# The weights of a row norm, its epsilons and the sums of its shares go from GpSimd to VectorE; GpSimd keeps the power

## The chip, the cores and the metric

The kernel runs on one core of one Trainium2 chip. The metric is the device time of one launch in microseconds (us), the median over runs; lower is better. The core has five engines that each work through a queue of their own, in the order in which it was written: TensorE (PE in the profile; PEld is its loading of weights), VectorE (DVE), ScalarE (ACT), GpSimd (POOL) and SyncE (SP), which here issues the DMAs. An engine starts its next instruction when the semaphores that this instruction waits for have been raised by others.

## The reference

A decoder trunk of two layers over 512 tokens, 1024 wide, all in float32. Each layer runs four parts in a row, and each part takes a row norm before and after:

```python
def rmsnorm(x, g):
    y = xf * lax.rsqrt(jnp.mean(xf * xf, axis=-1, keepdims=True) + RMS_EPS)
    return (y * g.astype(jnp.float32)).astype(x.dtype)

    f = swiglu(rmsnorm(h, g[0]), ...)          # gated FFN, 2816 wide
    h = h + FFN_RES_WEIGHT * rmsnorm(f, g[1])
    m_in = rmsnorm(h, g[2])                    # layer 0: retention, layer 1: stick-breaking attention
    h = h + rmsnorm(m, g[3])
    f = swiglu(rmsnorm(h, g[4]), ...)
    h = h + FFN_RES_WEIGHT * rmsnorm(f, g[5])
    gate = jax.nn.sigmoid(rmsnorm(h, g[6]) @ ple_w_gate[i])
    h = h + rmsnorm(gate * e, g[7])            # e: the layer's own input embedding, projected
```

So there are eight junctions in the program at which a part ends, is normed and added to the stream (the post norm and the residual), and the sum is normed again for the next part (the pre norm). After the last part there is no pre norm. Retention also norms each head, with an epsilon of its own.

## The kernel before

The 512 tokens are four blocks of 128 (t = 0 to 3), one token per partition. `part[t]` (in the rows below `part_92` to `part_95`, or `part`) holds a part's output of 128x1024 for block t, in two column halves a and b of 512. Matmuls run in float32r, each operand split into a high and a low piece (`wh` and `wl` for weights, `xs` for the turned input): ScalarE writes the high piece (L153), VectorE the low one (L150), and a product is three matmuls (L158 to L160, or L713 inside the FFN).

The end of a part is its *tail*. For each block the last matmuls of half a and then half b fall into PSUM (`ps`). What follows for block t, in the names used below:

- add a, add b (L552, L559 on VectorE): the half from PSUM is added into `part[t]`. In the input-embedding part, called PLE from here, a product with the sigmoid stands in their place (L1184).
- square a (L518, ScalarE): squares of half a with their row sum `ss`. Then, in `post_a`, epsilon a (L520) and weight a (L522), both on GpSimd: the epsilon is added to the sum, and half a is multiplied by the norm's weights `gbc`.
- square b (L532, ScalarE), weight b (L533, VectorE), and in `post_b` on GpSimd the sum of the two shares (L534) and the power -1/2 (L535).
- residual (L540, VectorE): `part[t]` times that power plus the old stream `rin`.
- the pre norm in `pre`: the square of the whole row (L459, ScalarE), epsilon and power in `rstd` (L450, L451, GpSimd), and the scaling into `xn` (L464, VectorE).
- turning: eight transposes of `xn` on TensorE (L471), then high and low pieces into `xs` (L153, L150).

In an FFN's tail the matmuls of a and b alternate block by block, twelve each. In retention and stick-breaking attention the four halves a are closed first, one after the other, and then half b block by block. In PLE half a comes from a product that is done before the tail, and the tail loads its weights (`blk<-raw`, home blocks) as it starts. Transposes of blocks 0 and 1 stand in TensorE's queue inside the tail, behind the matmuls of block 2 and behind the half a of block 3 (in retention and attention at the corresponding places), those of blocks 2 and 3 between matmuls of the next part on blocks 0 and 1.

The order of each queue is made when the program is built. TensorE's is the order of the code (`manual_schedule`). On the other engines a list scheduler picks by priority; everything in a tail stands in `chained` regions with high priority, and these tie the tail's instructions on VectorE, ScalarE and GpSimd to the order in which the code names them. So where the code names an instruction is where it stands in its engine's queue.

`rstd` is also called in retention for each head and block (L898 gives it a variance); there it stands between VectorE's statistics and a product on GpSimd (L902).

Of the kernel before, what the change touches and what calls it, by code (L numbers as in the profile page):

```python
# [15 lines left out]
ALU = mybir.AluOpType  # L16
# [13 lines left out]
RMS_EPS = 1e-6  # L30
# [47 lines left out]
class Trunk:  # L78
# [367 lines left out]


    def rstd(self, ss, eps):
        r = self.st()
        self.nc.gpsimd.tensor_scalar(out=r, in0=ss, scalar1=1.0, scalar2=eps, op0=ALU.mult, op1=ALU.add)  # L450
        self.power = self.nc.gpsimd.tensor_tensor(out=r, in0=r, in1=self.mhalf, op=ALU.pow)  # L451
        return r

# [58 lines left out]
    def post_a(self, t, g, half):  # L512

        nc = self.nc
        k = 1.0 / 16 if half else 1.0 / 32
        ss = self.st()
        a = self.part[t][:, :512]
        nc.scalar.activation(self.junk, a, AF.Square, scale=k, accum_out=ss)  # L518
        r = self.st()
        nc.gpsimd.tensor_scalar(out=r, in0=ss, scalar1=1.0, scalar2=(4 if half else 1) * RMS_EPS,  # L520
                                op0=ALU.mult, op1=ALU.add)
        nc.gpsimd.tensor_tensor(out=a, in0=a, in1=g[:, :512], op=ALU.mult)  # L522
        return r

    def post_b(self, t, g, half, ssa, after):


        nc = self.nc
        k = 1.0 / 16 if half else 1.0 / 32
        ss, r = self.st(), self.st()  # L530
        b = self.part[t][:, 512:]
        nc.scalar.activation(self.junk, b, AF.Square, scale=k, accum_out=ss)  # L532
        nc.vector.tensor_tensor(out=b, in0=b, in1=g[:, 512:], op=ALU.mult)  # L533
        nc.gpsimd.tensor_tensor(out=r, in0=ss, in1=ssa, op=ALU.add)  # L534
        nc.gpsimd.tensor_tensor(out=r, in0=r, in1=self.mhalf, op=ALU.pow)  # L535

        def residual():
            rin = self.rins.pop(0)
            for c in (slice(0, 512), slice(512, D)) if self.halves else (slice(0, D),):
                nc.vector.scalar_tensor_tensor(out=self.part[t][:, c], in0=self.part[t][:, c], scalar=r,  # L540
                                               in1=rin[:, c], op0=ALU.mult, op1=ALU.add)
            if t + 2 < NT:
                self.fetch_res(t + 2)
            after(t)

        self.todo_c.append(residual)
# [774 lines left out]
```

## Time and profile before

| | us |
|---|---|
| median of 3 runs | 2278.73 (2278.62 to 2280.29) |
| the profiled execution, its own time | 2279.08 |
| its span, first to last instruction | 2276.3 |
| TensorE busy | 2194.0 (96%) |
| VectorE busy | 1480.5 (65%) |
| ScalarE busy | 1004.3 (44%) |
| GpSimd busy | 236.0 (10%) |
| mean granted TensorE clock | 0.988 |

How to read the rows: a timeline row is start, duration, engine, line, operation, output and inputs, shape, count, and in brackets the idle time of the engine ahead of it with what ended it. A row of the view of groups has the count, the busy time, the mean in ns, and the idle time ahead. In the view of waits stand who waited for whom, us in total, times and the longest. A row of the view by windows has the stretch, its length, then the busy time (and number) on PE, PEld, DVE, ACT and POOL, the granted clock (1.00 is full), the share of the DMA engines and GB/s. ACTIVATION_READ_ACCUMULATOR is the end of a square: it writes the row sum.

### The profile page before, as it was taken

The numbers are of one execution on the slowest core, as the hardware profiler recorded it, in microseconds if no ns is written. First come the engines' busy times: TensorE is split into PE (matmuls) and PEld (weight loads), VectorE is DVE, ScalarE is ACT, GpSimd is POOL, SyncE is SP. The second block draws the span as 40 slices with busy tenths as digits, with TensorE's granted clock in tenths as the row PEclk, the third lists the DMA queues.
The fourth block names the chain that finished last, engine by engine and source line by source line (L and its number), as shares of the span: only waits on it lengthen the run. The fifth ranks groups of instructions, "written<-read, shape, count | busy, mean of one in ns | idle before, by whom it ended". The sixth has DMA issues, their size and how long they took to land.

```text
span 2276.3 us, 33005 instructions
## 1 busy us (share of the span) xinstructions
PE 2194.0 (96%) x13640; PEld 1974.0 (87%) x13640; DVE 1480.5 (65%) x1739; ACT 1004.3 (44%) x1468; POOL 236.0 (10%) x337
## 2 busy tenths in 40 slices
PE   7999999999999999999989999999999989999988
PEld 6999998888888899999868999998888889999976
DVE  7977666553544587766667877567554578776664
ACT  5544443332232355444454544344555445444452
POOL 0000002211111300000131000002221220000022
PEclk9999999999999999999999999999999999999999
DMA  5432335232222423323443332335212233332341
GB/s 208 130 111 94 99 125 166 79 116 75 97 75 67 159 94 121 103 93 102 148 153 126 109 113 94 102 113 170 78 58 73 84 112 111 103 102 93 126 134 56
DMA packets 69414, 248.81 MB, mean 109 GB/s; under 512 B 7952, under 2 KB 7952, under 8 KB 69264
## 3 DMA queue, kind: packets, MB, share of 16 engines
q1 hardware_dynamic: 69264, 246.72, 32.9%
q8 instruction: 106, 1.74, 0.3%
q14 instruction: 44, 0.36, 0.0%
HBM read 229.38 MB, written 17.30 MB: 108 GB/s over the span
## 4 chain that ended last, share of the span: by engine, by line
PE 85%; DVE 7%; ACT 3%; POOL 2%; issue 1%; DMA 1%; SPq 0%; DVEq 0%; POOLq 0%; ACTq 0%
PE ps L713 35%; PE ps L159 16%; PE ps L160 16%; PE ps L158 16%; PE ps L1018 1%; DVE part L540 1%; ACT xn L459 1%; POOL st L535 1%; DVE xs L150 1%; DVE wl L150 1%; DMA raw<-wts 1%; ACT wh L153 1%; ACT junk L532 1%; DVE xn L464 1%; POOL st L534 1%
## 5 line engine op out<-in xcount | busy, mean ns | idle before, releaser
L150 DVE TENSOR_TENSOR wl<-raw,wh 128x1024 fp32r<-128x1024 f32 x435 | 537.1, 1237 | 425.3 <-ACT wh L153 422.9
L153 ACT ACTIVATE wh<-raw 128x1024 fp32r<-128x1024 f32 x435 | 460.9, 1060 | 726.4 <-PE ps L160 229.3
L713 PE MATMUL ps<-xs,wh 128*128 128x256 f32 x2560 | 462.8, 282 | 0.0
L713 PEld LDWEIGHTS ps<-xs,wh 128*128 128x128 f32 x2560 | 399.1, 189 | 4.3 <-DVE y L676 0.2
L713 PE MATMUL ps<-xs,wl 128*128 128x256 f32 x1280 | 362.7, 283 | 0.0
L713 PE MATMUL ps<-xe,wh 128*128 128x256 f32 x1920 | 348.6, 283 | 0.0
L713 PEld LDWEIGHTS ps<-xe,wh 128*128 128x128 f32 x1920 | 300.3, 192 | 1.2
L158 PE MATMUL ps<-wh,blk 128*128 128x512 f32 x744 | 291.6, 392 | 1.5 <-DVE blk L904 1.5
L160 PE MATMUL ps<-wh,blk 128*128 128x512 f32 x744 | 291.1, 391 | 0.5 <-DVE blk L150 0.5
L159 PE MATMUL ps<-wl,blk 128*128 128x512 f32 x744 | 291.4, 392 | 0.0
L713 PE MATMUL ps<-xe,wl 128*128 128x256 f32 x960 | 271.6, 283 | 0.0
L713 PEld LDWEIGHTS ps<-xs,wl 128*128 128x128 f32 x1280 | 241.5, 189 | 0.0
L159 PE MATMUL ps<-xs,wh 128*128 128x256 f32 (+1 forms) x576 | 189.0, 328 | 12.4 <-DVE xs L150 12.4
L158 PE MATMUL ps<-xs,wh 128*128 128x256 f32 (+1 forms) x576 | 189.8, 329 | 4.7 <-ACT xs L153 4.7
L160 PE MATMUL ps<-xs,wl 128*128 128x256 f32 (+1 forms) x576 | 187.8, 326 | 0.0
L713 PEld LDWEIGHTS ps<-xe,wl 128*128 128x128 f32 x960 | 183.9, 192 | 0.0
L160 PEld LDWEIGHTS ps<-wh,blk 128*128 128x128 f32 x744 | 140.1, 188 | 30.6 <-DVE blk L150 0.9
L158 PEld LDWEIGHTS ps<-wh,blk 128*128 128x128 f32 x744 | 140.2, 188 | 29.1 <-DVE blk L904 1.9
L159 PEld LDWEIGHTS ps<-wl,blk 128*128 128x128 f32 x744 | 140.3, 189 | 27.1
L158 PE MATMUL ps<-wh,xs 128*128 128x512 f32 (+1 forms) x448 | 162.7, 363 | 0.1
L160 PE MATMUL ps<-wh,xs 128*128 128x512 f32 (+1 forms) x448 | 162.5, 363 | 0.0
L159 PE MATMUL ps<-wl,xs 128*128 128x512 f32 (+1 forms) x448 | 162.4, 363 | 0.0
(163 smaller groups left out, 3236.1 us busy)
## 6 DMA issues: line engine op xcount, KB each, us to landing
raw<-wts SPq DMA_DIRECT2D x382, 512.0 KB, 3.5
keep<-part SPq DMA_DIRECT2D x28, 512.0 KB, 4.4
rin<-keep SPq DMA_DIRECT2D x28, 512.0 KB, 4.1
gbc<-gains SPq DMA_DIRECT2D x16, 512.0 KB, 3.8
part<-x SPq DMA_DIRECT2D x4, 512.0 KB, 7.6
rin<-x SPq DMA_DIRECT2D x4, 512.0 KB, 5.3
out<-part SPq DMA_DIRECT2D x8, 256.0 KB, 2.1
dec<-decay SPq DMA_DIRECT2D x4, 256.0 KB, 3.9
```

Source lines behind the costliest of these rows:

```text
L150: eng.tensor_tensor(out=out, in0=x, in1=h, op=ALU.subtract)
L153: self.nc.scalar.activation(hl[0], x, AF.Copy)
L158: mm(ps, a[0], b[0], start=start, stop=False)
L159: mm(ps, a[0], b[1], start=False, stop=False)
L160: mm(ps, a[1], b[0], start=False, stop=stop)
L459: a = nc.scalar.activation(xn, self.part[t], AF.Square, scale=1.0 / 32, accum_out=ss)
L464: v = nc.vector.scalar_tensor_tensor(out=xn, in0=self.part[t], scalar=r, in1=g, op0=ALU.mult, op1=ALU.mult)
L532: nc.scalar.activation(self.junk, b, AF.Square, scale=k, accum_out=ss)
L534: nc.gpsimd.tensor_tensor(out=r, in0=ss, in1=ssa, op=ALU.add)
L535: nc.gpsimd.tensor_tensor(out=r, in0=r, in1=self.mhalf, op=ALU.pow)
L540: nc.vector.scalar_tensor_tensor(out=self.part[t][:, c], in0=self.part[t][:, c], scalar=r, in1=rin[:, c], op0=ALU.mult, op1=ALU.add)
L713: nc.tensor.matmul(o, w[a][:, g, k, :], x[b][:, k, :], start=new and g + k + n == 0, stop=k == 3 and n == 2, skip_group_check=True)
```

## The change

`post_a`'s product with the weights, every epsilon, and the sum of the two shares are issued to VectorE; the multiplication by one in front of each epsilon goes. In `post_a` the product now stands ahead of the epsilon. GpSimd keeps the power alone (and retention's own products and the masks of attention, which the change doesn't touch). `post_b` gets its sum and power through `rstd`.

```diff
     def rstd(self, ss, eps):
+
         r = self.st()
-        self.nc.gpsimd.tensor_scalar(out=r, in0=ss, scalar1=1.0, scalar2=eps, op0=ALU.mult, op1=ALU.add)
+        if isinstance(eps, float):
+            self.nc.vector.tensor_scalar(out=r, in0=ss, scalar1=eps, scalar2=None, op0=ALU.add)
+        else:
+            self.nc.vector.tensor_tensor(out=r, in0=ss, in1=eps, op=ALU.add)
         self.power = self.nc.gpsimd.tensor_tensor(out=r, in0=r, in1=self.mhalf, op=ALU.pow)
         return r
...
         nc.scalar.activation(self.junk, a, AF.Square, scale=k, accum_out=ss)
         r = self.st()
-        nc.gpsimd.tensor_scalar(out=r, in0=ss, scalar1=1.0, scalar2=(4 if half else 1) * RMS_EPS,
-                                op0=ALU.mult, op1=ALU.add)
-        nc.gpsimd.tensor_tensor(out=a, in0=a, in1=g[:, :512], op=ALU.mult)
+        nc.vector.tensor_tensor(out=a, in0=a, in1=g[:, :512], op=ALU.mult)
+        nc.vector.tensor_scalar(out=r, in0=ss, scalar1=(4 if half else 1) * RMS_EPS, scalar2=None, op0=ALU.add)
         return r
...
-        ss, r = self.st(), self.st()
+        ss = self.st()
         b = self.part[t][:, 512:]
         nc.scalar.activation(self.junk, b, AF.Square, scale=k, accum_out=ss)
         nc.vector.tensor_tensor(out=b, in0=b, in1=g[:, 512:], op=ALU.mult)
-        nc.gpsimd.tensor_tensor(out=r, in0=ss, in1=ssa, op=ALU.add)
-        nc.gpsimd.tensor_tensor(out=r, in0=r, in1=self.mhalf, op=ALU.pow)
+        r = self.rstd(ss, ssa)
```

The order on TensorE and SyncE stays as it was, row by row. On VectorE it changes in every tail. This is VectorE's queue in the tail of layer 0's second FFN, from block 0's half b to block 1's residual; first before, with the engine that each row waits for (Activation is ScalarE):

```order
L559 TENSOR_TENSOR part_92<-part_92,ps 128x512 [waits PE_49]
L533 TENSOR_TENSOR part_92<-part_92,gbc 128x512 [waits Activation_49]
L540 SCALAR_TENSOR_TENSOR part_92<-part_92,st,rin 128x1024 [waits DVE_49,Pool_49]
L552 TENSOR_TENSOR part_93<-part_93,ps 128x512 [waits PE_49]
L559 TENSOR_TENSOR part_93<-part_93,ps 128x512 [waits PE_49]
L533 TENSOR_TENSOR part_93<-part_93,gbc 128x512 [waits Activation_49]
L464 SCALAR_TENSOR_TENSOR xn<-part_92,st,gbc 128x1024 [waits Pool_49]
L540 SCALAR_TENSOR_TENSOR part_93<-part_93,st,rin 128x1024 [waits DVE_49,Pool_49]
```

and the same stretch in the changed program, whose line numbers are two to four higher:

```order
L561 TENSOR_TENSOR part_92<-part_92,ps 128x512 [waits PE_49]
L536 TENSOR_TENSOR part_92<-part_92,gbc 128x512 [waits Activation_49]
L454 TENSOR_TENSOR st<-st 128x1
L542 SCALAR_TENSOR_TENSOR part_92<-part_92,st,rin 128x1024 [waits Pool_49]
L452 TENSOR_SCALAR st<-st 128x1 [waits Activation_49]
L554 TENSOR_TENSOR part_93<-part_93,ps 128x512 [waits PE_49]
L524 TENSOR_TENSOR part_93<-part_93,gbc 128x512 [waits Activation_49]
L525 TENSOR_SCALAR st<-st 128x1
L561 TENSOR_TENSOR part_93<-part_93,ps 128x512 [waits PE_49]
L536 TENSOR_TENSOR part_93<-part_93,gbc 128x512 [waits Activation_49]
L454 TENSOR_TENSOR st<-st 128x1
L468 SCALAR_TENSOR_TENSOR xn<-part_92,st,gbc 128x1024 [waits Pool_49]
```

Between block 0's residual (L542) and block 1's add a (L554) there now stands the pre norm's epsilon (L452), which waits for ScalarE; and between add a and add b stand weight a and epsilon a, which wait for ScalarE too.

The second place is the start of layer 0's PLE tail, where four products with the sigmoid (`part<-blk`) are followed by the low pieces of the tail's weights (`blk<-raw,blk`, eight halves). Before:

```order
L1184 TENSOR_TENSOR part_94<-blk 128x512 [waits Activation_49]
L1184 TENSOR_TENSOR part_95<-blk 128x512 [waits DMAHW7_49,Activation_49]
L150 TENSOR_TENSOR blk<-raw,blk 128x512 [waits Activation_49] x4
L150 TENSOR_TENSOR blk<-raw,blk 128x512 [waits DMAHW5_49,Activation_49]
L150 TENSOR_TENSOR blk<-raw,blk 128x512 [waits Activation_49]
```

and now:

```order
L1186 TENSOR_TENSOR part_94<-blk 128x512 [waits Activation_49]
L524 TENSOR_TENSOR part_92<-part_92,gbc 128x512 [waits DMAHW6_49,Activation_49]
L525 TENSOR_SCALAR st<-st 128x1
L1186 TENSOR_TENSOR part_95<-blk 128x512 [waits DMAHW7_49,Activation_49]
L150 TENSOR_TENSOR blk<-raw,blk 128x512 [waits Activation_49]
L524 TENSOR_TENSOR part_93<-part_93,gbc 128x512 [waits Activation_49]
L525 TENSOR_SCALAR st<-st 128x1
L150 TENSOR_TENSOR blk<-raw,blk 128x512 [waits Activation_49]
```

The four weights a and epsilons a, which GpSimd worked through beside these rows, now stand among them. Outside the tails the scheduler moved a few rows past their neighbours at the start of three FFNs and once inside attention.

## The prediction

> **What bounds the kernel now.** First the page's shares and its chain of waits:
>
> ```profile
> PE 2194.0 (96%) x13640; PEld 1974.0 (87%) x13640; DVE 1480.5 (65%) x1739; ACT 1004.3 (44%) x1468; POOL 236.0 (10%) x337
> PE 85%; DVE 7%; ACT 3%; POOL 2%; issue 1%; DMA 1%; SPq 0%; DVEq 0%; POOLq 0%; ACTq 0%
> ```
>
> TensorE bounds it, and its work isn't changed. So the edit counts only where TensorE stands and waits for the norms. The view of waits names those places:
>
> ```profile
> PE ps L471 <- DVE xn L464: 27.2, 12, 8.1
> PE ps L159 <- DVE xs L150: 12.4, 8, 3.0
> ```
>
> The first row is the transposes that wait for the scaled row. The timelines of four FFN tails and of attention's tail show where it arises:
>
> ```profile
> 373.56 1.09 PE L471 MATMUL ps<-ident,xn 128*128 128x128 f32 x8 [2.08 <-DVE xn L464]
> 1144.20 1.09 PE L471 MATMUL ps<-ident,xn 128*128 128x128 f32 x8 [2.06 <-DVE xn L464]
> 1574.04 1.09 PE L471 MATMUL ps<-ident,xn 128*128 128x128 f32 x8 [2.08 <-DVE xn L464]
> 2198.23 1.09 PE L471 MATMUL ps<-ident,xn 128*128 128x128 f32 x8 [2.03 <-DVE xn L464]
> 1833.39 1.94 PE L471 MATMUL ps<-ident,xn 128*128 128x128 f32 x8 [3.50 <-DVE xn L464]
> ```
>
> In every FFN tail TensorE stands 2.0 to 2.1 us ahead of block 1's transposes: there the norm chain, not TensorE, sets the pace, and each us added to that chain is a us of the run.
>
> **The FFN tail.** The chain from block 0's residual to block 1's scaling, in the tail at 1130 us:
>
> ```profile
> 1130.61 1.28 DVE L540 SCALAR_TENSOR_TENSOR part<-part,st,rin 128x1024 f32<-128x1024 f32 x1 [0.71 <-POOL st L535]
> 1131.81 0.68 DVE L552 TENSOR_TENSOR part<-part,ps 128x512 f32<-128x512 f32 x1
> 1131.93 1.06 ACT L459 ACTIVATE xn<-part 128x1024 f32<-128x1024 f32 x1 [2.75 <-DVE part L540]
> 1132.90 0.18 ACT L459 ACTIVATION_READ_ACCUMULATOR xn<-part 128x1 f32 x1
> 1132.99 0.62 ACT L518 ACTIVATE junk<-part 128x512 bf16<-128x512 f32 x1
> 1133.51 0.19 ACT L518 ACTIVATION_READ_ACCUMULATOR junk<-part 128x1 f32 x1
> 1134.65 1.31 DVE L533 TENSOR_TENSOR part<-part,gbc 128x512 f32<-128x512 f32 x1 [0.85 <-ACT junk L532]
> 1135.88 1.27 DVE L464 SCALAR_TENSOR_TENSOR xn<-part,st,gbc 128x1024 f32<-128x1024 f32 x1
> 1136.08 1.48 POOL L535 TENSOR_TENSOR st<-st,mhalf 128x1 f32<-128x1 f32 x1
> 1137.60 1.29 DVE L540 SCALAR_TENSOR_TENSOR part<-part,st,rin 128x1024 f32<-128x1024 f32 x1 [0.44 <-POOL st L535]
> 1142.87 1.27 DVE L464 SCALAR_TENSOR_TENSOR xn<-part,st,gbc 128x1024 f32<-128x1024 f32 x1
> ```
>
> Before, VectorE runs add a (1131.81) while ScalarE squares the row, and epsilon a and weight a run on GpSimd beside it. One residual to the next takes 1137.60 - 1130.61 = 6.99 us, and to block 1's scaling 1142.87 - 1130.61 = 12.26.
>
> With the change VectorE's queue has the epsilon ahead of add a, and weight a ahead of add b; each waits for ScalarE, and everything of block 1 is queued behind. Counted from the residual's start, with these rows: the row's square is read out at 1132.90 + 0.18 = 1133.08, so at 2.47; epsilon at 2.50. No 128x1 operation of VectorE is in the trace. The nearest rows:
>
> ```profile
> L898 DVE BATCH_NORM_AGGREGATE st<-st 128x2 f32<-128x6 f32 x16 | 2.9, 182 | 0.6
> L872 DVE TENSOR_TENSOR sc<-ps,dec 128x256 f32<-128x256 f32 x4 | 1.7, 418 | 0.0
> L872 DVE TENSOR_TENSOR sc<-ps,dec 128x128 f32<-128x128 f32 x4 | 1.1, 281 | 0.0
> ```
>
> From 256 to 128 columns 137 ns go; another 128 leave 0.14 to 0.15, of which the next instruction overlaps some 0.08 (L464 starts at 1135.88, L533 ends at 1135.96). I take 0.07 in the queue; bounds are 0 and the 0.18 of the first row. So add a starts at 2.57 and ends 0.69 later; hop to ScalarE 0.04; square of a half 0.71 (1132.99 to 1133.70); hop back 0.03: weight a at 4.04. Its length is 0.69, of which 0.61 hold the queue; epsilon a 0.07: add b at 4.72, then 0.69 + 0.04 + 0.71 + 0.03: weight b at 6.19; the sum at 6.80; scaling of the block before at 6.87. The power waits until the scaling has ended, as it does now: L535 began at 1136.08 but ended 0.41 after L464's end. So the next residual stands at 6.87 + 1.27 + 0.41 + 0.04 = 8.59 in place of 6.99, and block 1's scaling at 8.59 + 6.87 = 15.46 in place of 12.26. **The wait of 2.1 us becomes 5.3: +3.2 in each of four tails, +12.8.** (With the bounds of the 128x1 operations, three per block, 11.5 to 15.4.) Block 0's residual itself stays: its sum now follows weight b on VectorE, but on GpSimd it also ended with weight b.
>
> Block 2: after two low pieces the residual and add a come as before (the epsilon's wait lies under that of the pieces), add a 4.2 us behind the residual. From there the new order takes 0.73 + 0.71 + 0.03 + 0.68 + 0.73 + 0.71 + 0.03 + 0.68 = 4.3 to the scaling, before 3.5. These 0.8 us are paid where TensorE waits for block 2, ahead of the two PLE parts: **+1.6**. In the other two tails the transposes come 0.95 behind the scaling's end, as here, so 0 (at most 1.6 more):
>
> ```profile
> 382.29 1.27 DVE L464 SCALAR_TENSOR_TENSOR xn<-part,st,gbc 128x1024 f32<-128x1024 f32 x1
> 384.51 1.03 PE L471 MATMUL ps<-ident,xn 128*128 128x128 f32 x8
> ```
>
>
> What the change gives back is the shared access of VectorE and GpSimd: L533 above took 1.31 for 0.69, as it waited for weight a on GpSimd. That is in the sum already. The Trainium skill (SBUF — State Buffer, Who interferes with whom) has it as a lock on the port pair: a VectorE instruction with two inputs in SBUF and a GpSimd instruction that reads SBUF exclude each other, and the one that comes second blocks. The rows agree (1.31, 1.48), and by that rule alone the change would be a gain, the first rival below.
>
> **Retention and attention.**
>
> ```profile
> 764.44 2.73 DVE L552 TENSOR_TENSOR part<-part,ps 128x512 f32<-128x512 f32 x4 [1.08 <-PE ps L160]
> 771.92 0.69 DVE L559 TENSOR_TENSOR part<-part,ps 128x512 f32<-128x512 f32 x1 [4.75 <-PE ps L160]
> 784.95 1.28 DVE L464 SCALAR_TENSOR_TENSOR xn<-part,st,gbc 128x1024 f32<-128x1024 f32 x1
> 786.28 0.98 PE L471 MATMUL ps<-ident,xn 128*128 128x128 f32 x7
> 1819.05 2.73 DVE L552 TENSOR_TENSOR part<-part,ps 128x512 f32<-128x512 f32 x4 [2.82 <-PE ps L160]
> 1828.24 1.28 DVE L540 SCALAR_TENSOR_TENSOR part<-part,st,rin 128x1024 f32<-128x1024 f32 x1 [3.89 <-POOL st L535]
> 1833.68 1.29 DVE L540 SCALAR_TENSOR_TENSOR part<-part,st,rin 128x1024 f32<-128x1024 f32 x1 [0.44 <-POOL st L535]
> 1837.41 1.28 DVE L464 SCALAR_TENSOR_TENSOR xn<-part,st,gbc 128x1024 f32<-128x1024 f32 x1
> ```
>
> Four halves a were closed in 2.73 us on VectorE. Now each takes 0.69 + 0.04 + 0.71 + 0.03 + 0.61 + 0.07 = 2.15, together 8.6. In retention block 0's add b would start at 773.04, not 771.92 (+1.1); in block 1, add b follows the epsilon rather than the residual, and its scaling comes 4.72 behind the residual (6.87 less the 2.15 of a), where it took 3.73 (1837.41 - 1833.68 in attention, and alike here): +1.0. Its transposes have no slack (784.95 + 1.28 = 786.23 against 786.28): **+2.1**. In attention GpSimd's four weights a had held up the residual (3.89 above); 1819.05 + 8.6 + 2.98 = 1830.63 is still later than 1828.24, +2.4. Then +1.0 to the next residual (6.44 for 5.44) and +1.0 to the scaling (4.72 for 3.73): **+4.4**.
>
> **The PLE tail** gains:
>
> ```profile
> 1186.64 1.66 DVE L1184 TENSOR_TENSOR part<-blk 128x512 f32<-128x512 f32 x1 [0.40 <-ACT blk L1183]
> 1188.23 8.16 DVE L150 TENSOR_TENSOR blk<-raw,blk 128x512 fp32r<-128x512 f32 x8
> 1187.18 0.50 PE L158 MATMUL ps<-blk,xs 128*128 128x512 f32 x1 [1.60 <-ACT blk L153]
> 1188.96 0.50 PE L159 MATMUL ps<-blk,xs 128*128 128x512 f32 x1 [1.28 <-DVE blk L150]
> ```
>
> Eight low pieces take 8.16 us, 1.02 each, since weight a on GpSimd alternates with them. Alone they cost 0.61 each. Now L1184 ends at 1187.33, the last piece starts 7 x 0.61 + 3 x 0.68 = 6.3 later and ends at 1194.2; before 1196.4. **-1.8 in each of two, -3.6** (-0.6 if TensorE is at half clock there, at most -2.6).
>
> The rows that the scheduler moved at the heads of FFNs and in attention: 0, within 2 either way (a piece later or earlier by one or two rows of 0.6). Retention's epsilons save about 0.1 each off the path: 0.
>
> **The clock.**
>
> ```profile
> 374.00:378.00 4.00, 4.00 (x15) 3.22 (x14) 2.30 (x4) 2.07 (x4) 0.74 (x2) 0.61 0.33 121
> 1144.00:1148.00 4.00, 3.80 (x21) 3.31 (x22) 2.53 (x4) 1.43 (x3) 0.74 (x2) 1.00 0.16 65
> 1833.00:1837.00 4.00, 3.61 (x13) 3.25 (x14) 2.33 (x4) 1.99 (x5) 1.33 (x3) 0.50 0.56 170
> ```
>
> After the gap of 2.08 at 373 the granted clock fell to half, after the same gap at 1144 it didn't (nor at 1574 and 2198, by the same view); after 3.50 it stayed down for all of the 4 us. Gaps of 5.3 should bring it in all four FFN tails. In the first row 0.39 x 4 = 1.6 us were lost; three new ones, less some 0.5 of later short waits that they swallow: **+3.5** (0 to 10). The Trainium skill (TensorE: Matmul & The Clock Gate, The HAM clock gate) says that a whole idle window of about 3.4 us on a free-running grid throttles to half. By it a gap of 2 could never do it, though the trace shows one that did; a gap of 5.3 could miss a whole window too, so an estimate from that page would put the term between 0 and 5.
>
> **The sum.** 12.8 + 1.6 + 2.1 + 4.4 - 3.6 + 0 + 3.5 = 20.8 us on the profiled execution's 2279.08 gives 2299.9; that execution lies 0.35 above the median shown, so **2299.5**.
>
> **Rivals.**
> - *Relief of the shared access decides: faster.* Place: weight b, the power, and attention's first residual. Price: 0.62 of L533 per block, twice per FFN tail (-5.0), attention -3.5 (TensorE's gap there, as the residual's wait of 3.89 goes), PLE -3.6: 12.1 less, 2267. For: the rows of 1.31 and 8.16. Against: it needs VectorE not to stand on the squares, and the queue puts a waiting epsilon ahead of add a. It decides only if a block's period stays under 6.99; mine is 8.59. 0.05.
> - *No change.* The longer gap is taken from waits that come later (12.4 us in all on `xs`). Against: these wait for the same chain, they move with it. 2279, 0.04.
> - *The clock makes it much worse.* With gaps of 5 to 7 us each of six tails stays at half for 6.8 us, as attention's nearly does: 6 x 3.4 = 20 less the 4 it already pays and some 3 swallowed, +13 for my 3.5: 2309 and more. 0.21.
>
> **Chances.** My forecast has 0.70, with its own range 2289 to 2306 (the ends of the 128x1 price, the moved rows and PLE's gain). With the clock rival above and a little of the others below: 2287 to 2312. Changes under 0.2% (4.6 us) can't be told from none. Faster 0.05, same 0.04, slower 0.91.
>
> **What would show it.** VectorE's epsilon of the pre norm waits about 1.2 us for ScalarE in nearly every block, weight a 0.8; residual to residual is 8.6 in FFN tails; transposes of block 1 wait about 5.3 in four FFN tails and the total of L471 on xn goes from 27 to near 48; weight b takes 0.69 each; the eight pieces in PLE end two us earlier; GpSimd falls from 236 to some 154 us; the clock shows a dip behind each FFN tail. I'd be wrong if the period stays at 7, if add a starts ahead of the epsilon, or if a 128x1 operation costs well over 0.18.

## The result, and the profile after

The changed kernel takes 2305.24 us (median of 4 runs, 2303.82 to 2306.21), the kernel before 2278.89 beside it: a ratio of 1.0110, 95% interval 1.0098 to 1.0122. By the medians it is **26.4 us slower**. The forecast was 2299.5, so its sign was right and its 20.8 us were 5.6 too few.

The page of the changed kernel: busy time, and the chain that ended last.

```profile
PE 2201.3 (96%) x13640; PEld 1976.5 (86%) x13640; DVE 1495.3 (65%) x1883; ACT 1005.2 (44%) x1468; POOL 155.1 (7%) x193
PE 80%; DVE 10%; issue 4%; ACT 4%; POOL 2%; DMA 0%; SPq 0%; ACTq 0%; POOLq 0%; DVEq 0%
```

GpSimd fell from 236.0 to 155.1 us, VectorE grew by only 15, though it got 22.1 of weights (L524) and 17.0 of 128x1 operations (L452, L454, L525): its own operations are held up by GpSimd less. TensorE's share of the chain went from 85 to 80%, VectorE's from 7 to 10. Work isn't what was added to the end; waits are. The view of waits (total us, times, longest):

```profile
PE ps L475 <- DVE xn L468: 46.8, 18, 7.9
DVE st L452 <- ACT xn L463: 40.7, 30, 5.6
DVE part L536 <- ACT junk L535: 29.3, 32, 2.2
DVE part L524 <- ACT junk L522: 19.5, 23, 1.1
```

The first row is the one that stood at 27.2 us before. The second and the last are new: the pre norm's epsilon (L452) and weight a (L524) now stand at the head of VectorE's queue until ScalarE has squared. How that goes into one block is seen in VectorE's timeline in the tail at 1140 us (the brackets: time idle before, and what ended it):

```profile
1140.13 1.28 DVE L542 SCALAR_TENSOR_TENSOR part<-part,st,rin 128x1024 f32<-128x1024 f32 x1 [0.73 <-POOL st L455]
1142.63 0.15 DVE L452 TENSOR_SCALAR st<-st 128x1 f32<-128x1 f32 x1 [1.22 <-ACT xn L463]
1142.70 0.68 DVE L554 TENSOR_TENSOR part<-part,ps 128x512 f32<-128x512 f32 x1
1144.23 0.69 DVE L524 TENSOR_TENSOR part<-part,gbc 128x512 f32<-128x512 f32 x1 [0.85 <-ACT junk L522]
1144.84 0.15 DVE L525 TENSOR_SCALAR st<-st 128x1 f32<-128x1 f32 x1
1144.90 0.68 DVE L561 TENSOR_TENSOR part<-part,ps 128x512 f32<-128x512 f32 x1
1146.45 0.69 DVE L536 TENSOR_TENSOR part<-part,gbc 128x512 f32<-128x512 f32 x1 [0.87 <-ACT junk L535]
1147.06 0.15 DVE L454 TENSOR_TENSOR st<-st 128x1 f32<-128x1 f32 x1
1147.13 1.28 DVE L468 SCALAR_TENSOR_TENSOR xn<-part,st,gbc 128x1024 f32<-128x1024 f32 x1
1148.85 1.28 DVE L542 SCALAR_TENSOR_TENSOR part<-part,st,rin 128x1024 f32<-128x1024 f32 x1 [0.44 <-POOL st L455]
1153.24 0.69 DVE L524 TENSOR_TENSOR part<-part,gbc 128x512 f32<-128x512 f32 x1 [1.15 <-ACT junk L522]
1156.12 1.28 DVE L468 SCALAR_TENSOR_TENSOR xn<-part,st,gbc 128x1024 f32<-128x1024 f32 x1
```

Three times per block VectorE idles (1.22, 0.85, 0.87). In the first two an add of block 1, whose matmuls are done, stands queued behind; the third, ahead of weight b, was there before as well (0.85). Residual to residual is 1148.85 - 1140.13 = 8.72 us (before 6.99, forecast 8.59). On TensorE:

```profile
370.12 1.09 PE L475 MATMUL ps<-ident,xn 128*128 128x128 f32 x8 [0.43 <-DVE xn L468]
378.80 1.54 PE L475 MATMUL ps<-ident,xn 128*128 128x128 f32 x6 [4.84 <-DVE xn L468]
1148.46 1.09 PE L475 MATMUL ps<-ident,xn 128*128 128x128 f32 x8 [0.54 <-DVE xn L468]
1157.45 1.97 PE L475 MATMUL ps<-ident,xn 128*128 128x128 f32 x8 [5.12 <-DVE xn L468]
```

Block 1's transposes wait 4.8 to 5.1 us in each FFN tail, where they waited 2.0 to 2.1, and block 0's, which hadn't waited, stand 0.4 to 0.55 (the other two tails: 0.55 and 4.87, 0.54 and 4.87). Set one against the other, matmul by matmul, the kernel loses 5.6, 7.1, 4.6 and 5.7 us in the four FFN tails (23.0 of the 27.2 by which the span grew), 2.4 in retention's tail, 4.6 in attention's, and gains 3.2 and 1.9 in the two PLE parts.

The clock is the other difference. Summing (1 - granted clock) over windows of 1 us, 38.3 us are lost to it in the changed kernel's span and 27.4 in that of before: 10.9 more. (A stretch of 3.4 us at half clock loses 1.7 in this sense.)

### The profile page after: what moved, and what is told of

Read it like the earlier page. It is cut to its first block, busy times and chain, and to the rows that moved or that the text cites. A ratio compares the mean times of both kernels' runs of the same rounds, so it can differ in the third digit from the quotient of the medians.

```text
span 2303.5 us, 32927 instructions
## 1 busy us (share of the span) xinstructions
PE 2201.3 (96%) x13640; PEld 1976.5 (86%) x13640; DVE 1495.3 (65%) x1883; ACT 1005.2 (44%) x1468; POOL 155.1 (7%) x193
## 4 chain that ended last, share of the span: by engine, by line
PE 80%; DVE 10%; issue 4%; ACT 4%; POOL 2%; DMA 0%; SPq 0%; ACTq 0%; POOLq 0%; DVEq 0%
PE ps L715 34%; PE ps L159 15%; PE ps L160 15%; PE ps L158 15%; PE ps L1020 2%; DVE wl L150 1%; DVE part L542 1%; POOL st L455 1%; ACT xn L463 1%; DVE xs L150 1%; ACT junk L535 1%; PE ps L475 1%; DVE blk L244 1%; DVE part L536 1%; ACT wh L153 1%
## 5 line engine op out<-in xcount | busy, mean ns | idle before, releaser
L159 PE MATMUL ps<-xs,wh 128*128 128x256 f32 (+1 forms) x576 | 185.9, 323 | 11.4 <-DVE xs L150 11.3
L158 PE MATMUL ps<-xs,wh 128*128 128x256 f32 (+1 forms) x576 | 187.4, 325 | 5.1 <-ACT xs L153 5.1
L455 POOL TENSOR_TENSOR st<-st,mhalf 128x1 f32<-128x1 f32 x80 | 63.1, 789 | 1900.2 <-DVE st L454 1567.5
```

What stands on the lines that cost most here:

```text
L158: mm(ps, a[0], b[0], start=start, stop=False)
L159: mm(ps, a[0], b[1], start=False, stop=False)
```

## Experiments

Two theories were set against each other. **Theory 1, the forecast's**: what costs is a waiting instruction at the head of VectorE's queue, with add a or add b behind it. **Theory 2**: what costs is the added work itself, wherever it stands. A second question came with the result: are the 5.6 us that the forecast lacks due to the chain or to the clock?

### The same work, without the waits

```diff
-    post_a:  square a; vector weight a; vector epsilon a
-    post_b:  square b;                                    vector weight b; rstd
+    post_a:  square a
+    post_b:  square b; vector weight a; vector epsilon a; vector weight b; rstd
     pre:
-        r = self.rstd(ss, RMS_EPS)
+        r = self.st()
+        nc.gpsimd.tensor_scalar(out=r, in0=ss, scalar1=1.0, scalar2=RMS_EPS, op0=ALU.mult, op1=ALU.add)
+        self.power = nc.gpsimd.tensor_tensor(out=r, in0=r, in1=self.mhalf, op=ALU.pow)
```

> The pre norm's epsilon is back on GpSimd, and weight a with its epsilon stays on VectorE but is issued behind square b, ahead of weight b. VectorE has the same operations as the changed kernel, less 32 epsilons of 128x1 (under 5 us of the whole); no waiting instruction stands ahead of add a or add b. By the rows of before, counted from block 0's residual: add a 1.20, add b 1.81, square a 2.38 to 3.09, square b to 3.80, weight a 3.12, weight b 3.83, sum 4.44, scaling 4.51, next residual 4.51 + 1.27 + 0.45 = 6.23. THEORY 1 (waits at the head of VectorE's queue): the period is 6.2, shorter than the 6.99 of before, so -0.76 x 2 x 4 = -6.1 in the FFN tails, -3.6 in the two PLE tails, -3.5 in attention; with 0 to -3 for the clock 2264 us (2258 to 2269), FASTER than before. THEORY 2 (the added work on VectorE itself, wherever it stands): as the changed kernel, 2300 to 2306.

Measured: 2264.98 us (2263.65 to 2266.44), ratio to before 0.9932 (0.9917 to 0.9947). **Faster than both kernels**, with VectorE busy for 1491.3 us where the changed kernel has 1495.3. Theory 2 falls. VectorE's timeline in the same tail (in this kernel add a is L556, add b L563, weight a L536, weight b L538, the residual L544):

```profile
1131.52 1.28 DVE L544 SCALAR_TENSOR_TENSOR part<-part,st,rin 128x1024 f32<-128x1024 f32 x1 [0.66 <-POOL st L455]
1132.72 0.68 DVE L556 TENSOR_TENSOR part<-part,ps 128x512 f32<-128x512 f32 x1
1133.98 0.69 DVE L563 TENSOR_TENSOR part<-part,ps 128x512 f32<-128x512 f32 x1 [0.59 <-PE ps L160]
1134.63 0.69 DVE L536 TENSOR_TENSOR part<-part,gbc 128x512 f32<-128x512 f32 x1
1135.54 0.69 DVE L538 TENSOR_TENSOR part<-part,gbc 128x512 f32<-128x512 f32 x1 [0.16 <-ACT junk L534]
1137.95 1.28 DVE L544 SCALAR_TENSOR_TENSOR part<-part,st,rin 128x1024 f32<-128x1024 f32 x1 [0.44 <-POOL st L455]
```

Add a follows the residual at once, and the waits of 1.22 and 0.85 are gone. The period is 1137.95 - 1131.52 = 6.43 (forecast 6.23; add b had to wait 0.59 for TensorE, so here TensorE sets part of the pace). The view of waits tells the same:

```profile
PE ps L477 <- DVE xn L470: 21.3, 13, 7.9
DVE part L538 <- ACT junk L534: 5.5, 22, 0.6
DVE part L536 <- ACT junk L524: 3.3, 7, 0.6
```

Transposes wait 21.3 us in all (46.8 in the changed kernel, 27.2 before).

### One wait at a time

The same two edits, each alone. First only the pre norm's epsilon back on GpSimd (the last four lines of the diff above):

> The changed kernel with only the pre norm's epsilon back on GpSimd: the wait ahead of add a goes, that of weight a ahead of add b stays. From block 0's residual: add a 1.20, square a 2.38 to 3.09, weight a 3.12, epsilon, add b 3.80, square b from 4.53 to 5.24, weight b 5.27, sum 5.88, scaling 5.95, next residual 7.67. THEORY 1: +0.68 x 2 x 4 = +5.4 over before in FFN tails, +1 to +2 in block 2 and in retention, +3.5 in attention, -3.6 in PLE: +8; with 2 to 6 for the clock 2290 us (2285 to 2296), about half of the change's loss. THEORY 2: the epsilon's own 0.07 x 32 is all that goes: 2303 to 2305.

Measured: 2291.92 us (2290.96 to 2293.18), ratio to before 1.0051 (1.0034 to 1.0068). Then only weight a and its epsilon behind square b (the other lines):

> The changed kernel with weight a and its epsilon issued behind square b; the pre norm's epsilon stays on VectorE, ahead of add a. The wait ahead of add b goes, that ahead of add a stays. From block 0's residual: add a 2.57, add b 3.18, square a to 4.01, square b to 4.72, weight a 4.04, weight b 4.75, sum 5.36, scaling 5.43, next residual 7.15. THEORY 1: +0.16 x 2 x 4 = +1.3 in FFN tails, -3.6 in PLE, -3.5 in attention: -6, with 0 to 3 for the clock 2274 us (2269 to 2280), so the early weight a alone carries over 20 of the change's 26 us. THEORY 2: as the changed kernel, 2304 to 2306, since VectorE does the very same operations.

Measured: 2278.20 us (2275.6 to 2284.76), ratio 0.9994 (0.9985 to 1.0004): as before. This kernel has the very same operations on every engine as the changed one (VectorE is busy for 1495.9 us, there for 1495.3), and 27.0 us less. Its view of waits:

```profile
DVE st L452 <- ACT xn L463: 40.7, 30, 5.5
PE ps L475 <- DVE xn L468: 31.6, 14, 8.0
DVE part L534 <- ACT junk L522: 4.2, 11, 1.6
```

The epsilon still waits 40.7 us; weight a (here L534) 4.2 in place of 19.5. Each set against the kernel before that ran with it, the four kernels stand at +26.4 (both waits), +11.3 (weight a's alone), -2.4 (the epsilon's alone) and -15.6 (neither). Taking away the epsilon's wait is worth 15.1, weight a's 28.8, both 42.0: within 2 us they add. The second includes attention, where the four weights a had stretched the four adds of half a from 2.73 to 8.75 us; here they take 2.73 again.

### One part of the change alone

Epsilons and sums on VectorE, weight a left on GpSimd:

```diff
     post_a of the changed kernel:
-        nc.vector.tensor_tensor(out=a, in0=a, in1=g[:, :512], op=ALU.mult)
+        nc.gpsimd.tensor_tensor(out=a, in0=a, in1=g[:, :512], op=ALU.mult)
```

> One part of the change alone: epsilons and sums are on VectorE, weight a stays on GpSimd. Two epsilons stand in VectorE's queue ahead of work that could run: that of the pre norm ahead of add a, epsilon a ahead of add b. From block 0's residual by the rows of before: add a 2.57, square a to 4.01, epsilon a 4.04, add b 4.11, square b to 5.55, weight b 5.58, sum 6.19, scaling 6.26, next residual 7.98. THEORY 1 (waits at the head of VectorE's queue): +0.99 for the period and as much again for the scaling, x 4 = +7.9; retention, attention and block 2 +1 each; nothing gained in PLE, where weight a still alternates with the low pieces on GpSimd: +11, with 0 to 3 for the clock and up to 3 less in moved rows 2291 us (2286 to 2296), although only 128x1 operations moved. THEORY 2 (the length of the added work): three operations of 0.07 per block, 32 blocks, under 7 us if every one were on the path: 2279 to 2285.

Measured: 2294.95 us (2293.81 to 2299.11), ratio 1.0067 (1.0052 to 1.0082): +15.0 from operations of 128x1 alone, which take 17 us of VectorE in the whole kernel. It lies at the upper end of what theory 1 gave. The other part alone, weight a on VectorE in the place where the change has it, epsilons and sums on GpSimd:

```diff
     post_a of the kernel before:
-        nc.gpsimd.tensor_tensor(out=a, in0=a, in1=g[:, :512], op=ALU.mult)
+        nc.vector.tensor_tensor(out=a, in0=a, in1=g[:, :512], op=ALU.mult)
```

> The other part alone: weight a is on VectorE where the change put it, epsilons and sums stay on GpSimd. From block 0's residual: add a 1.20, square a 2.38 to 3.09, weight a 3.12, add b 3.73, square b to 5.17, weight b 5.20, scaling 5.81, next residual 7.53. THEORY 1: +0.54 x 2 x 4 = +4.3, block 2 and retention +1 each, attention +3, PLE -3.6: +6, with 0 to 4 for the clock 2287 us (2283 to 2292). So both parts cost less alone (some 11 and 8) than together (26): in the change the second wait starts only when the first has ended, and the longer gaps reach the clock. THEORY 2 (the length of the added work, 0.61 x 32 = 19.5 us, is what counts): nearly all of the change's loss, 2298 to 2305.

Measured: 2288.65 us (2287.69 to 2289.49), ratio 1.0037 (1.0024 to 1.005): +8.7. Both parts lose by themselves, 15.0 + 8.7 = 23.7 of the 26.4. That they would cost much more together than apart, as I had expected (11 and 8), is not borne out.

### The smallest edit that wins

```diff
     post_a of the kernel before:
-        nc.gpsimd.tensor_tensor(out=a, in0=a, in1=g[:, :512], op=ALU.mult)
     post_b, behind square b:
+        a = self.part[t][:, :512]
+        nc.vector.tensor_tensor(out=a, in0=a, in1=g[:, :512], op=ALU.mult)
         nc.vector.tensor_tensor(out=b, in0=b, in1=g[:, 512:], op=ALU.mult)
```

> The kernel before with one edit: weight a goes from GpSimd to VectorE, issued behind square b and ahead of weight b; epsilons and sums stay on GpSimd. By the rows as in the kernel with the late weight and the late epsilon, less 0.07 per 128x1 operation that VectorE no longer has. THEORY 1: 2263 us (2259 to 2268), as that kernel (2264.98) or 1 to 2 better: where the epsilons and sums run is worth next to nothing once nothing waits ahead of the adds. RIVAL (GpSimd's 128x1 operations are what the chain pays for, 0.19 for each epsilon in a row of before): the late weight gives its gain only with the sums on VectorE, 2268 to 2273.

Measured: 2265.26 us (2264.69 to 2267.18), ratio 0.9935 (0.9921 to 0.995). As with epsilon a and the sums on VectorE (2264.98). The rival falls: where these 128x1 operations run is worth nothing that can be measured, once nothing waits ahead of the adds. The whole difference between this kernel and the one with weight a early (2288.65) is the place of one instruction in VectorE's queue: 23.4 us.

Where the gain over the kernel before arises is another matter. Block 1's transposes wait only 0.74 us in the FFN tails, for 2.0 to 2.1 before. Yet, set matmul by matmul, the four FFN tails together gain only 1.4 of the 12.6 us by which the span shrinks; the two PLE parts gain 4.6 and attention's tail 3.3. In this trace the clock falls at the end of all four FFNs, before only at one, so much of what the shorter chain gives there is lost again at half clock.

### The clock

Is the part that the forecast lacks the clock's? First its dips behind block 1's gap were taken away:

```diff
     tail of the changed kernel, FFN only, last block, ahead of block 1's transposes:
+        fill = self.ps()
+        for i in range(32):
+            nc.tensor.transpose(fill[:, i % 4 * P : i % 4 * P + P], self.ident, self.ident)
         self.flush(0)
```

> The changed kernel with 32 transposes of the identity (128x128, 0.136 us each by L471's rows, 4.4 us together) put on TensorE ahead of block 1's transposes in the four FFN tails, where it now stands 4.8 to 5.1 us. They compute nothing that is used. The chain on VectorE stays, so what changes is that TensorE does not stand idle there. THEORY A (the clock is the part that was sized too small): the granted clock does not fall behind the FFN tails (in the trace of the changed kernel it fell for 6.8 us behind three of four, and 3.4 us in one), some 10 us at half clock less, so about 5 to 8 us less than the changed kernel: 2298 us (2296 to 2301). THEORY B (the FFN tails grew by more than forecast because the chain itself is longer than reckoned, and the clock's falls are paid in waits anyway): no change against the changed kernel, 2304 to 2306.

Measured: 2302.84 us (2301.36 to 2303.83), ratio to before 1.0098 (1.0083 to 1.0113). That is 2.4 us less than the changed kernel (4.1 if each is set against the kernel before that ran with it), between the two theories, and the intervals of the two ratios overlap: by itself it decides nothing. The clock did as wanted: it no longer fell right behind block 1's gap, and 31.3 us were lost to it in place of 38.3. But of these 7.0 us of clock only 2 to 4 came back in time. (In the trace of the changed kernel it had fallen for 6.8 us there in all four tails, not in three as the expectation has it.) In the tail at 1150 us block 2's transposes wait 2.02 us where they waited 0.66: the time that TensorE spent at half clock it now spends waiting, since VectorE's chain comes no sooner (and the clock falls behind this wait instead, at 1166 us). So what is lost to the clock can't simply be added to the time of the run.

While looking for where the clock falls, I laid windows of one dip's length, 3.41 us, end to end over the traces. All dips of one run (a dip is a stretch at half clock) begin on one such grid. Here are windows of the changed kernel on its grid (length, busy time of PE, PEld, DVE, ACT and POOL, granted clock, DMA share, GB/s):

```profile
349.68:353.09 3.41, 1.47 (x7) 0.86 (x5) 1.95 (x3) 1.63 (x3) 0.00 (x0) 1.00 0.60 177
353.09:356.51 3.42, 3.42 (x9) 2.49 (x8) 0.99 (x2) 0.23 (x1) 0.00 (x0) 0.50 0.35 131
373.57:376.99 3.42, 0.39 (x2) 0.00 (x0) 1.72 (x5) 1.68 (x5) 0.27 (x1) 1.00 0.78 277
376.99:380.40 3.41, 1.60 (x8) 1.60 (x9) 3.41 (x6) 0.74 (x2) 1.46 (x1) 0.50 0.00 0
380.40:383.81 3.41, 3.41 (x10) 2.73 (x9) 1.86 (x4) 2.12 (x4) 0.55 (x1) 0.50 0.55 187
383.81:387.23 3.42, 3.42 (x26) 3.22 (x26) 2.26 (x5) 0.94 (x3) 0.00 (x0) 1.00 0.67 213
```

A window with TensorE busy for 1.47 of 3.41 is followed by one at half; one with 0.39 likewise, and as the next has only 1.60 the half clock lasts a second window. To test this reading, TensorE's wait of 1.94 us for ScalarE at the start of each FFN's last part, which all kernels here have, was filled in the last kernel:

```diff
     tail, FFN only, block 0, ahead of the third group of three matmuls:
+        fill = self.ps()
+        for i in range(12):
+            nc.tensor.transpose(fill[:, i % 4 * P : i % 4 * P + P], self.ident, self.ident)
```

> The late weight with GpSimd's epsilons and sums, and 12 transposes of the identity (1.6 us, unused) on TensorE in the wait of 1.94 us with which each FFN's last part begins. THEORY (the granted clock halves for 3.41 us behind every window of 3.41 us, on a grid that is fixed within a run, in which TensorE was busy for less than half): a wait of 1.94 leaves a window less than half busy wherever over 1.71 of it falls in one window, so in some 2 or 3 of 4 FFN tails; with 1.6 of it filled, none. No half clock just behind those four places, where the trace of the late weight with its epsilon had it at 352, 1123, 1550 and 2168 us; 1.7 us less for each: 4 to 7 us less than without the filling, 2259 us (2255 to 2262). RIVAL (the clock falls by something other than TensorE's idle time, or the time is then lost in the next wait): no change against the kernel without the filling, within 2 us.

Measured: 2258.18 us (2257.7 to 2259.57), ratio to before 0.9905 (0.9888 to 0.9921), the fastest of all: 7.1 us less than without the filling. The windows at the first two FFN ends, without it:

```profile
348.50:351.91 3.41, 1.47 (x6) 0.63 (x4) 2.24 (x3) 1.34 (x3) 0.00 (x0) 1.00 0.61 196
351.91:355.33 3.42, 3.42 (x9) 2.68 (x9) 0.69 (x2) 0.52 (x1) 0.00 (x0) 0.50 0.30 111
1119.91:1123.33 3.42, 1.83 (x7) 1.23 (x8) 1.57 (x3) 0.63 (x1) 0.00 (x0) 1.00 0.67 243
1123.33:1126.74 3.41, 3.41 (x10) 2.63 (x9) 0.69 (x1) 0.72 (x2) 0.19 (x1) 0.50 0.03 10
```

and with it:

```profile
349.78:353.19 3.41, 2.77 (x17) 2.02 (x16) 1.91 (x3) 0.63 (x1) 0.00 (x0) 1.00 0.77 265
1117.78:1121.19 3.41, 2.77 (x18) 1.98 (x17) 2.25 (x3) 0.91 (x3) 0.00 (x0) 1.00 0.68 216
1121.19:1124.61 3.42, 3.42 (x17) 2.79 (x15) 0.69 (x1) 0.73 (x2) 0.19 (x1) 1.00 0.19 78
```

The half clock is gone behind all four, and here it is paid nearly in full: set matmul by matmul, the four places give 1.54, 1.59, 1.57 and 1.62 us, 6.3 for 4 x 1.7 = 6.8, since TensorE has 19 us of matmuls ahead of it and waits for nobody. (The 12 transposes fill 1.3 us, not 1.6: 0.64 of each wait is left.) The rest of the half clock is another matter. Over the whole trace 25.8 us are lost without the filling and 11.0 with it; of the 8.0 that went elsewhere, little came back in time.

Last, the two kernels of the case with these fillings, to see the chain apart from the clock: the changed one with both, the one before with the 12 alone (there the gap of 2.1 was left).

> The changed kernel with both fillings of TensorE: the 32 unused transposes in the wait ahead of block 1, and the 12 in the wait of 1.94 us with which each FFN's last part begins. To be set against the kernel before with the 12 alone: the two then differ by the norm chain, with the half clock at the FFNs' ends taken out of both. THEORY A (the forecast's terms of the chain, 17.3 us, are right, and the clock is what was sized too small): 16 to 19 us between the two. THEORY B (the chain's terms were too small as well: block 0's transposes now wait too, 0.4 to 0.55 in each tail, and so do the heads of the FFNs): 20 to 23 us between them. This kernel itself: 2302.8 with the first filling alone, less 1.7 for each of the three FFN ends at which the clock fell, 2298 us (2294 to 2301).

> The kernel before with the 12 unused transposes in the wait of 1.94 us with which each FFN's last part begins. In its trace the clock fell behind that wait in one of four tails (2177 us), and behind block 1's gap of 2.08 in one other (374 us), where the rest of that window was no full cover. THEORY (a window under half busy halves the clock for the next): 1.7 to 3.5 us less than before, and about the same gain whether or not the norms are changed: 2277 us (2274 to 2279). RIVAL: the half clock at these places is lost in a later wait and costs nothing, 2279 to 2281.

Measured: 2296.34 us (2294.52 to 2298.35), ratio to before 1.0070 (1.0053 to 1.0087), and 2276.92 (2274.81 to 2277.85), ratio 0.9984 (0.9975 to 0.9994). The times are as expected, and the distance of 19.4 us lies between the two theories' ranges: it decides for neither. Nor is it the chain alone, since the clock isn't out of these two: 21.5 us are still lost to it in the changed kernel and 29.0 in the one before, so here it works for the changed one. In the one before the time came as forecast, but not for the reason given, and that is luck: the dip at the FFN's end (2177) is gone, but others came, and its trace loses 29.0 us where it lost 27.4 without the filling (granted clock over its runs 0.986 to 0.988, without the filling 0.987 to 0.989). Why it is 2.9 us faster stays open.

## Why the prediction was right, and where it was short

**Right: what decides.** Two instructions that wait for ScalarE were put ahead of ready work on VectorE, and it was the waits that cost, not the work: set against the kernel before, the same operations in another order are 28.8 us faster, and with one epsilon back on GpSimd 42.0.

**The FFN tail, forecast +3.2 each.** The steps came out as reckoned, counted from the residual at 1140.13: epsilon 2.50 (forecast 2.50), add a 2.57 (2.57), weight a 4.10 (4.04), add b 4.77 (4.72), weight b 6.32 (6.19), scaling 7.00 (6.87), next residual 8.72 (8.59). In the second block weight a came 4.39 behind its residual, not 4.10 (the 1.15 above): ScalarE's square a started 0.39 after add a had ended (1152.10), and the trace has it wait for GpSimd's power, a wait that the forecast had not reckoned with. Block 1's scaling stood at 15.99, not 15.46.

```profile
1152.49 0.63 ACT L522 ACTIVATE junk<-part 128x512 bf16<-128x512 f32 x1 [1.17 <-POOL st L455]
```

Between the two filled kernels block 1's transposes fall back by 3.5, 3.9, 3.6 and 3.6 us, 14.5 in all for my 12.8. I also took block 0 as unchanged. Its residual is, but its scaling goes from 1135.88 - 1130.61 = 5.27 behind the residual to 7.00, and with 1.2 of slack (the transposes stood at 1138.36, the scaling's end at 1137.15) that makes the 0.4 to 0.55 of wait at block 0's transposes. It is part of the 3.2, not on top of it, so the sum was right without the step.

**128x1 operations.** 0.15 us each, of which 0.07 hold the queue (1142.63 to 1142.70), as taken.

**Block 2, forecast +1.6.** Ahead of the two PLE parts TensorE fell back by 1.9 and 2.2 us between the two original traces, and in the other two tails, which I had at 0, by 0.8 and 1.1 behind block 1. But this is half clock: block 2's transposes wait 0.66 us there, less than before (0.88 and 0.84). Between the two filled kernels, where the half clock behind block 1 is gone from the changed one, they wait 2.02 for 0.88 and 0.59. So the chain grew by 1.1 and 1.4 for my 0.8 each, and in the original trace the slow clock hid it.

**Retention +2.1, attention +4.4.** 2.4 and 4.6: right, and by the steps that were reckoned. Four halves a take 8.75 us in both (forecast 8.6), the scaling stands 4.78 behind the residual (4.72).

**PLE, forecast -3.6.** VectorE's row there shows what was expected, the low pieces no longer alternating with GpSimd:

```profile
1206.31 3.09 DVE L150 TENSOR_TENSOR blk<-raw,blk 128x512 fp32r<-128x512 f32 x5
```

The last piece ends at 1209.40, where with the lag of 15.1 us at this place it would have ended at 1196.39 + 15.1 = 1211.5: 2.1 earlier. In time the two PLE parts gained 3.2 and 1.9, but 1.7 of the first is a dip of the clock that one trace has there and the other hasn't.

**Moved rows, forecast 0.** The FFN's head behind the first PLE part lost 1.3, those behind retention and attention some 0.5 each, where TensorE now waits 0.45 and 0.58: together a little over the 2 that were allowed.

**The clock, forecast +3.5, and what the 5.6 us are.** The trace has 10.9 us more lost to half clock, but not all of that is paid. TensorE's busy time, with the same matmuls, grew by 2201.3 - 2194.0 = 7.3 us and its idle time by the rest of the span's 27.2, 19.9, where the sum had 3.5 and 17.3. That adds up what happened, but doesn't separate the two, since time at half clock can be time that TensorE would otherwise have waited. The filled kernels don't separate them either. An estimate: the filled gap brought back 2.4 to 4.1 us for 7.0 of clock, the last kernel 7.1 for 14.8, so about half is paid. By that the clock's part of the 26.4 is some 5, and the chain's 21 by the original pair (26.4 less half of 10.9) or 23 by the filled one (19.4 and half of 7.5). So most of the missing 5.6 would be the chain's: block 1's transposes in the FFN tails 1.7, block 2 0.9, the heads of the FFNs 1 or more. The clock's share would be up to 2. No run here settles this split.

For the clock's dips, the reckoning itself was too simple. It took them from block 1's gaps alone, 1.6 each. But a gap of 4.8 us leaves the next window short of work too and holds the half clock for 6.8, and each shift of the program against the grid can put other waits, such as the 1.94 at the FFNs' ends, into one window. The rule that the prediction quoted from the Trainium skill (TensorE: Matmul & The Clock Gate, The HAM clock gate) has its window's length and free-running grid confirmed by these traces (below); that the window must be idle as a whole they contradict: windows with TensorE busy for 43% of the time sufficed (1.47 of 3.41 above).

**The rivals.** The relief of the shared access was real: weight b went from 923 ns to 692 on the mean, and the low pieces of `raw` from 953 to 681. First the kernel before, then the changed one:

```profile
L533 DVE TENSOR_TENSOR part<-part,gbc 128x512 f32<-128x512 f32 x32 | 29.5, 923 | 31.2 <-ACT junk L532 31.2
L536 DVE TENSOR_TENSOR part<-part,gbc 128x512 f32<-128x512 f32 x32 | 22.2, 692 | 29.3 <-ACT junk L535 29.3
```

The move became a gain as soon as no wait stood ahead of the adds (2265.26). The rule of the Trainium skill (SBUF — State Buffer, Who interferes with whom) that was named beside it holds here, and what decided the sign was the place in the queue. The much worse clock, 2309 and more, didn't come, though 10.9 us more were lost to it, two thirds of the 16 (20 less 4) that this rival reckoned with. Where the chain is late anyway, a slow TensorE costs less: only 2.4 to 4.1 of 7.0 us in the filled gap.

## What to carry to other kernels

When work moves to an engine that has room, look at what it waits for and at what stands behind it in that engine's queue: an epsilon that takes 0.07 us and waits 1.2 in front of ready work cost some 15 us over the kernel. Place the moved instruction behind the work that is ready: weight a alone went from +8.7 us to -14.7 that way. And look at TensorE's idle time window by window: a short wait just ahead of a long stretch of matmuls can cost nearly twice its length (1.94 us, and about 1.6 more at half clock).

## What the chip showed that I had not expected

The granted clock follows a rule that can be read from these traces. In twelve of them (all kernels here), windows of 3.413 us were laid from the first dip's edge; every dip behind the first 24 us began on its run's grid, within 0.03 us over 1800 us, and the grid's offset from the start of the span differs from run to run (2.80, 1.53, 0.97, 0.34, ...). Of 7733 windows at full clock, leaving out the first 24 us, TensorE was busy for less than 44% in 139: all 139 were followed by a window at half clock. In 7543 it was busy for more than 54%: two were. Between lie 51, of which 24 were. Of 183 windows at half clock, 28 had TensorE busy for less than 80%, and in all 28 the half clock went on; of the other 155 it went on in two. The ends of TensorE's matmuls in the profile are modelled, so the two bounds are near a half and near four fifths, no more exact. It also explains the case that had puzzled me in the trace of before, where the same gap of 2.08 us lowered the clock once and three times not: the one fell whole into a window, the others across an edge.

```profile
371.43:374.84 3.41, 1.33 (x11) 1.25 (x11) 3.41 (x5) 0.34 (x1) 2.40 (x3) 1.00 0.49 191
374.84:378.25 3.41, 3.41 (x10) 2.66 (x9) 1.71 (x3) 2.12 (x4) 0.74 (x2) 0.50 0.46 156
1139.43:1142.84 3.41, 2.70 (x12) 1.88 (x10) 2.02 (x3) 2.94 (x8) 2.60 (x5) 1.00 0.85 246
1142.84:1146.25 3.41, 2.05 (x13) 1.88 (x14) 3.41 (x5) 0.00 (x0) 1.63 (x2) 1.00 0.16 66
```

In the first row the gap leaves 1.33 of 3.41 and the next window is at half; in the last two the same gap takes 0.71 of one window and 1.36 of the next, and both are followed by full clock.
